# Pairing the value and gate projections: seven block products in place of eight on half of the k-tiles

## The chip, the cores and the metric

The kernel runs on one core of a Trainium2 chip. That core has five engines that run side by side, each working through its own list of instructions strictly in order: TensorE (PE) for matrix products, VectorE (DVE) and ScalarE (ACT) for elementwise work, GpSimd (POOL) and SyncE (SP), which here mostly issue DMA transfers. PE loads a stationary block of 128x128 (PEld in the profile) and streams a moving block of up to 512 columns past it; it accumulates into PSUM, which DVE and ACT read back into SBUF. The metric is the device time of one execution in microseconds, lower being better.

## The reference, cut to what matters

A sequence of 256 tokens of width 2048 passes through two layers. Each layer normalises the tokens, multiplies them by a wide input matrix, mixes over time per head, multiplies by a SiLU gate and projects back to 2048.

```python
# layer 0: gated linear attention, 4 heads
proj = h @ w_in                       # (256 x 2048) @ (2048 x 10240)
q, k, v, gate = jnp.split(proj, [1024, 2048, 2048 + 4096], axis=-1)
...                                   # decays, scores, o = scores @ v, per-head norm
return (o * jax.nn.silu(gate)) @ w_out            # (256 x 4096) @ (4096 x 2048)
# layer 1: retention, 8 heads
proj = h @ w_in                       # (256 x 2048) @ (2048 x 12288)
q, k, v, gate = jnp.split(proj, [2048, 4096, 4096 + 4096], axis=-1)
...                                   # rotary, scores * dmat, o = scores @ v, group norm
return (o * jax.nn.silu(gate)) @ w_out
```

All of it is float32. Nearly all of the arithmetic is in the four large products.

## The kernel before, in words

**Weights.** The host cuts the weights into groups of 512 columns; each group is 2048 rows, that is 16 k-tiles of 128 rows (`NKT`). A DMA on SP brings four k-tiles at a time into a tile `raw` (1 MB, three buffers, L110 to L118). To keep float32 accuracy with a one-pass matmul each weight is written as hi + lo: for two k-tiles at a time (a *sub*, `SUB` = 2, eight subs in a group), ACT copies the weights into `hi` with rounding (L151) and DVE subtracts, `lo = raw - hi` (L152), each an instruction over 128x1024 elements. `hi` and `lo` have three buffers each, and `LOOK` = 2 subs are split ahead of the one that PE is multiplying. The tokens are kept in the same form in `xhl` and `ogt`. A product is then three matmuls, hi·hi, hi·lo and lo·hi (`mm3`, L184 to L186).

**Groups.** `group_x` (L188) multiplies one weight group: for each sub, 2 k-tiles x 2 halves of 128 tokens x 3 matmuls of 512 columns, 12 in all, into two PSUM banks, one per half. `group_w` (L203) does the query and key group of a head, with weights stationary; its four results are brought back by `evac_w` (ACT L230, DVE L231).

**Heads.** A GLA head (`gla_head`, L575) has one `group_w`, then value group, gate group, value group, gate group. The value result is split into hi and lo by `v_evac` (L406, L407), the gate result goes through SiLU in `g_evac` (L415). A retention head (`ret_head`, L819) has one `group_w`, one value group and one gate group. After every two GLA heads and every four retention heads, `out_half` (L668) multiplies the gated output in `ogt` by four output groups and adds the result to `resid`, which stays in SBUF during the whole run.

**Order.** The smaller work (the decay and the scores of GLA `gla_scores`, L483; rotary and scores of retention `ret_scores`, L784; transposes `transpose_out`) is written as generators in a queue `side`; one step of it is taken after each sub by `advance`, and `drain_side` empties the queue at fixed places. `o_mms` (L418) multiplies scores by values, in a hook inside a later group. A scheduler that works on a timeline of its own then fixes the order on each engine; on the chip each engine follows that list and waits where an operand is not ready. PSUM is shared out as four banks `acc`, two `lev`, two `mis`.

Of the kernel before, what the change touches and what calls it, by code (L numbers as in the profile page):

```python
# [17 lines left out]
P = 128  # L18
# [7 lines left out]
CHUNK = 4  # L26
LOOK = 2
DMA_LOOK = 2
# [25 lines left out]

@with_exitstack
def kernel(
# [20 lines left out]
    raw_p = pool("raw", 3)  # L77
# [6 lines left out]
    sc_p = pool("sc", 2)  # L84
# [3 lines left out]
    acc_p = pool("acc", 4, space=psum)  # L88
    lev_p = pool("lev", 2, space=psum)
    mis_p = pool("mis", 2, space=psum)  # L90

# [6 lines left out]
    n_groups = w_all.shape[0]  # L98
    raws, splits = {}, {}
    emitted = {"raw": 0, "sub": 0}  # L100
    per_raw = CHUNK // SUB
    raws_per_group = NKT // CHUNK

    last0 = (n_groups - 1) * NSUB

    def emit_raw(parts=1):
        c = emitted["raw"]
        if c >= n_groups * raws_per_group:
            return
        t = raw_p.tile([P, CHUNK, GW], F32, tag="raw", name=f"raw{c}")  # L110
        g, j = divmod(c, raws_per_group)
        src = w_all[g, :, j * CHUNK * GW : (j + 1) * CHUNK * GW].rearrange("p (k n) -> p k n", n=GW)
        step = CHUNK // parts
# [24 lines left out]

    def emit_split(pieces=1):
        i = emitted["sub"]  # L140
        if i >= n_groups * NSUB:
            return
        c, j = divmod(i, per_raw)
        while emitted["raw"] <= min(c + DMA_LOOK, n_groups * raws_per_group - 1):
            emit_raw()
        src = raws[c][:, j * SUB : (j + 1) * SUB, :]
        hi, lo = split_tiles(i)
        step = SUB // pieces
        for k in range(pieces):
            sl = slice(k * step, (k + 1) * step)  # L150
            nc.scalar.activation(hi[:, sl], src[:, sl], AF.Copy)  # L151
            nc.vector.tensor_tensor(lo[:, sl], src[:, sl], hi[:, sl].bitcast(F32), ALU.subtract)  # L152
        splits[i] = (hi, lo)
        if j == per_raw - 1:
            del raws[c]
        emitted["sub"] += 1
# [17 lines left out]
    def next_weights():  # L174
        i = state["sub"]
        while emitted["sub"] <= min(i + LOOK, n_groups * NSUB - 1):
            emit_split()
        state["sub"] += 1
        return splits.pop(i)
# [8 lines left out]
    def group_x(lhs, name, hook=None, deadline=None, bank=None):  # L188
        bank = bank or (acc_p, "acc")
        ps = [bank[0].tile([P, GW], F32, tag=bank[1], name=f"{name}_ps{t}") for t in range(2)]  # L190
        for j in range(NSUB):
            if j == deadline:
                drain_side()
            hi, lo = next_weights()
            for q in range(SUB):
                for t in range(2):
                    mm3(ps[t], lhs, j * SUB + q, t, hi, lo, q)
            if hook is not None:
                hook(j)
            advance()  # L200
        return ps

    def group_w(rhs, name, extra=None):  # L203
        ps = [acc_p.tile([P, 2, SEQ], F32, tag="acc", name=f"{name}_ps{c}") for c in range(4)]
        for j in range(NSUB):
# [3 lines left out]
            if last:  # L209
                order = [(q, c) for c in range(4) for q in range(SUB)]  # L210
# [40 lines left out]
    resid = const([P, 2, D], "resid")  # L251
# [43 lines left out]
    w0 = emit_raw(4)  # L295
# [4 lines left out]
    w0(2)  # L300
    w0(3)
    x1 = load_xt(1)
    x1(0, 2)
    w1 = emit_raw(2)
    w1(0)
    x1(2, 4)
    w1(1)
    wa1_src = t4_p.tile([P, NKT, 16], F32, tag="qk", name="wa1_src", bufs=1)
    nc.sync.dma_start(wa1_src, w_a1)
    load_xt(2)(0, 4)  # L310
    emit_raw()
# [21 lines left out]
    def square_sum(t, c):  # L333
        junk = sg_p.tile([P, GW], F32, tag="sg", name="sqj")
        nc.scalar.activation(
            junk, resid[:, t, c * GW : (c + 1) * GW], AF.Square, accum_out=ssum[:, t, c : c + 1]
        )
# [5 lines left out]
    def first_group(j):  # L343
# [5 lines left out]
        if j == 1:  # L349
            load_xt(3)(0, 4)  # L350
        if j == 6:
# [22 lines left out]
    def gate_low_rank():  # L374
        for t in range(2):
            keep(nc.sync.dma_start(resid[:, t, :], x_n[:, t, :]))
            yield
        for c in range(8):
            square_sum(c // 4, c % 4)
            if c % 2:  # L380
                yield
# [21 lines left out]
    def v_evac(ps, r2, name):  # L403
        v = v_p.tile([P, 2, 2, GW], F32R, tag="v", name=name)
        for t in range(2):
            nc.scalar.activation(v[:, t, 0, :], ps[t], AF.Copy, scale=r2[:, t : t + 1])  # L406
            nc.vector.scalar_tensor_tensor(  # L407
                v[:, t, 1, :], ps[t], r2[:, t : t + 1], v[:, t, 0, :].bitcast(F32), ALU.mult, ALU.subtract
            )
        return v  # L410

    def g_evac(ps, r, name):
        sg = sg_p.tile([P, 2, GW], F32, tag="sg", name=name)
        for t in range(2):
            keep(nc.scalar.activation(sg[:, t, :], ps[t], AF.Silu, scale=r[:, t : t + 1]))  # L415
        return sg

    def o_mms(sc, v, name):  # L418
        ps = [acc_p.tile([P, GW], F32, tag="acc", name=f"{name}_ps{t}") for t in range(2)]
# [155 lines left out]
    def gla_head(h):  # L575
# [22 lines left out]
        def o_part(gi):  # L598
# [4 lines left out]
            o = o_p.tile([P, 2, GW], F32, tag="o", name=f"go{g}")  # L603
# [3 lines left out]
            os_.append(o)  # L607
# [28 lines left out]
        for gi in range(2):  # L636
            g = 2 * h + gi

            def v_hook(j):
                if h > 0 and gi == 1 and j == 1:  # L640
                    o_part(0)

            def g_hook(j):
                if h == 0 and gi == 1 and j == 5:
                    o_part(0)
                if gi == 1 and j == (6 if h == 0 else 2):
                    o_part(1)
# [4 lines left out]
            pv = group_x(xhl, f"gv{g}", v_hook)  # L652
            vs.append(v_evac(pv, r2, f"gv{g}"))
            sgs.append(g_evac(group_x(xhl, f"gg{g}", g_hook), r, f"gsg{g}"))
# [3 lines left out]
    def out_cols(c, ps, t, first, final):  # L658
        dst = resid[:, t, c * GW : (c + 1) * GW]
# [8 lines left out]
    def out_half(first, final, name):  # L668
        for c in range(4):
# [10 lines left out]
            for _ in transpose_out(  # L680
# [6 lines left out]
                pass  # L687

# [9 lines left out]
    def out_tail():  # L698
        kept = []
        half = GW // 2  # L700
        base = 3 * GW
        keep(nc.scalar.preload_act_table_set("natural_log_exp_and_others"))
        for t in range(2):
# [3 lines left out]
            ps = [acc_p.tile([P, half], F32, tag="acc", name=f"tail_ps{t}{n}") for n in range(2)]  # L707
# [111 lines left out]
    def ret_head(h):  # L819
# [11 lines left out]
        v = v_evac(group_x(xhl, f"rv{h}", bank=(lev_p, "lev")), r2, f"rv{h}")  # L831
# [5 lines left out]
        def o_part(j):  # L837
            if j != 2:
                return
            drain_side()  # L840
            po = o_mms(hw["sc"], v, f"ro{h}")
            o = o_p.tile([P, 2, GW], F32, tag="o", name=f"ro{h}")
# [18 lines left out]
            hw["o"] = o  # L861

        sg = g_evac(group_x(xhl, f"rg{h}", o_part), r, f"rsg{h}")
# [55 lines left out]
def _layout(i):  # L919
    gw, go = i["gla_w_in"][0], i["gla_w_out"][0]  # L920
    rw, ro = i["ret_w_in"][0], i["ret_w_out"][0]
    groups = []

    def add(a):
        groups.append(a.reshape(NKT, P, GW).transpose(1, 0, 2))

    def add_out(w, half):
        for c in range(4):
            add(w[half * D : (half + 1) * D, c * GW : (c + 1) * GW])

    for half in range(2):
        for h in (2 * half, 2 * half + 1):
            add(np.concatenate([gw[:, h * 256 : (h + 1) * 256], gw[:, 1024 + h * 256 : 1024 + (h + 1) * 256]], 1))
            for g in (2 * h, 2 * h + 1):
                add(gw[:, 2048 + g * GW : 2048 + (g + 1) * GW])
                add(gw[:, 6144 + g * GW : 6144 + (g + 1) * GW])
        add_out(go, half)
    for half in range(2):
        for h in range(4 * half, 4 * half + 4):
            add(np.concatenate([rw[:, h * 256 : (h + 1) * 256], rw[:, 2048 + h * 256 : 2048 + (h + 1) * 256]], 1))  # L940
            add(rw[:, 4096 + h * GW : 4096 + (h + 1) * GW])
            add(rw[:, 8192 + h * GW : 8192 + (h + 1) * GW])
        add_out(ro, half)
    w_all = np.empty((len(groups), P, NKT, GW), np.float32)
    for n, g in enumerate(groups):
        w_all[n] = g
# [14 lines left out]
        "w_all": w_all.reshape(len(groups), P, NKT * GW),  # L961
# [30 lines left out]
```

## Time and profile before

| what | value |
|---|---|
| time, median of 2 runs | 1443.36 us (1443.23 to 1443.49) |
| span of the profiled execution, first to last instruction | 1441.2 us |
| what lies around the span, median less span | 2.2 us |
| PE busy | 1429.9 us, 99% |
| DVE busy | 910.3 us, 63% |
| ACT busy | 690.0 us, 48% |
| DMA | 266.72 MB, mean 185 GB/s |
| granted TensorE clock, mean | 0.999 |

The busy times say what share of the span an engine had something under way. PE's matmuls overlap in the pipeline, so the duration of one matmul is longer than its share of the time: what one costs is the distance from one start to the next. In the groups of instructions each row has the line of the kernel, the engine, the operation, the written and the read tiles, the shape, the count, the busy time, the mean duration of one in ns, and the idle time just before with what ended it.

### The profile page before, as it was taken

To read this page: it belongs to the slowest core of one execution; us is meant where nothing else is said; L and a number is where in the kernel's file an instruction comes from. 1 tells how busy PE (TensorE), PEld (TensorE's weight loads), DVE (VectorE), ACT (ScalarE), POOL (GpSimd) and SP (SyncE) were. 2 spreads that over 40 slices of the span, in tenths; PEclk is the share of its full clock that TensorE was granted. 3 is DMA by queue.
4 is the path that set the end of the run, shared out by engine and by line. 5 is a ranking of instruction groups with operands and counts; after the bars stand their busy time and mean duration, and the time that the engine had idled before them with its cause. 6 is when DMAs were issued, how large, how long until landed. Compare 5 with 4: busy or idle time off the path is not lost.

```text
span 1441.2 us, 17504 instructions
## 1 busy us (share of the span) xinstructions
PE 1429.9 (99%) x6800; PEld 1181.0 (82%) x6800; DVE 910.3 (63%) x1430; ACT 690.0 (48%) x889; POOL 44.1 (3%) x98
## 2 busy tenths in 40 slices
PE   9999999999999999999999999999999999999997
PEld 6788888888888888888888888888888888888887
DVE  7595785545845764655666666664546666666654
ACT  4665654533554645454444444444344444444443
POOL 0010010000000010000000000000000000000000
PEclk9999999999999999999999999999999999999999
DMA  8643554555545555555555555555555555554562
GB/s 288 250 170 135 206 178 154 189 184 182 177 170 177 183 183 176 175 175 180 192 187 191 188 183 195 178 193 178 197 180 181 194 179 199 176 204 170 202 207 93
DMA packets 40499, 266.72 MB, mean 185 GB/s; under 512 B 4880, under 2 KB 5392, under 8 KB 9696
## 3 DMA queue, kind: packets, MB, share of 16 engines
q1 hardware_dynamic: 37536, 257.57, 51.2%
q0 software_dynamic: 2160, 6.95, 1.4%
q8 instruction: 53, 0.87, 0.2%
q10 hardware_dynamic: 720, 1.09, 0.2%
q14 instruction: 30, 0.25, 0.0%
HBM read 263.49 MB, written 2.10 MB: 184 GB/s over the span
## 4 chain that ended last, share of the span: by engine, by line
PE 99%; DMA 0%; SPq 0%; DVE 0%; ACT 0%; issue 0%
PE rqk_ps L219 8%; PE gv_ps L184 4%; PE gg_ps L185 4%; PE rv_ps L186 4%; PE gg_ps L186 4%; PE rv_ps L185 4%; PE rg_ps L185 4%; PE gv_ps L186 4%; PE rg_ps L186 4%; PE gv_ps L185 4%; PE rv_ps L184 4%; PE gg_ps L184 4%; PE rg_ps L184 4%; PE rqk_ps L220 4%; PE gqk_ps L219 4%; PE ra_ps L186 2%
## 5 line engine op out<-in xcount | busy, mean ns | idle before, releaser
L152 DVE TENSOR_TENSOR lo<-raw,hi 128x1024 fp32r<-128x1024 f32 (+1 forms) x473 | 577.6, 1223 | 439.9 <-ACT hi L151 421.5
L151 ACT ACTIVATE hi<-raw 128x1024 fp32r<-128x1024 f32 (+1 forms) x473 | 499.4, 1057 | 640.0 <-PE rg_ps L186 77.9
L219 PE MATMUL rqk_ps<-xhl,hi 128*128 128x512 f32 x480 | 165.9, 394 | 0.0
L220 PE MATMUL rqk_ps<-xhl,lo 128*128 128x256 f32 x480 | 127.2, 281 | 0.0
L219 PEld LDWEIGHTS rqk_ps<-xhl,hi 128*128 128x128 f32 x480 | 88.9, 188 | 16.1
L185 PE MATMUL gg_ps<-lo,xhl 128*128 128x512 f32 x256 | 102.1, 399 | 0.0
L185 PE MATMUL rv_ps<-lo,xhl 128*128 128x512 f32 x256 | 102.0, 399 | 0.0
L185 PE MATMUL gv_ps<-lo,xhl 128*128 128x512 f32 x256 | 102.0, 398 | 0.0
L186 PE MATMUL gv_ps<-hi,xhl 128*128 128x512 f32 x256 | 101.9, 398 | 0.0
L186 PE MATMUL gg_ps<-hi,xhl 128*128 128x512 f32 x256 | 101.7, 397 | 0.0
L186 PE MATMUL rv_ps<-hi,xhl 128*128 128x512 f32 x256 | 101.4, 396 | 0.0
L186 PE MATMUL rg_ps<-hi,xhl 128*128 128x512 f32 x256 | 101.3, 396 | 0.0
L185 PE MATMUL rg_ps<-lo,xhl 128*128 128x512 f32 x256 | 101.3, 396 | 0.0
L184 PE MATMUL gv_ps<-hi,xhl 128*128 128x512 f32 x256 | 94.7, 397 | 0.0
L184 PE MATMUL rv_ps<-hi,xhl 128*128 128x512 f32 x256 | 93.5, 396 | 0.0
L184 PE MATMUL rg_ps<-hi,xhl 128*128 128x512 f32 x256 | 93.5, 396 | 0.0
L184 PE MATMUL gg_ps<-hi,xhl 128*128 128x512 f32 x256 | 93.3, 397 | 0.0
L220 PEld LDWEIGHTS rqk_ps<-xhl,lo 128*128 128x128 f32 x480 | 89.2, 189 | 3.5
L219 PE MATMUL gqk_ps<-xhl,hi 128*128 128x512 f32 x240 | 80.0, 402 | 0.6 <-ACT hi L151 0.6
L220 PE MATMUL gqk_ps<-xhl,lo 128*128 128x256 f32 x240 | 57.6, 282 | 0.8 <-DVE lo L152 0.8
L186 PEld LDWEIGHTS rg_ps<-hi,xhl 128*128 128x128 f32 x256 | 48.1, 188 | 11.6
L185 PEld LDWEIGHTS rg_ps<-lo,xhl 128*128 128x128 f32 x256 | 48.1, 188 | 11.5
(265 smaller groups left out, 2395.2 us busy)
## 6 DMA issues: line engine op xcount, KB each, us to landing
raw<-in_w_all SPq DMA_DIRECT2D x238, 1024.0 KB, 4.8
resid<-in_x_n SPq DMA_DIRECT2D x2, 1024.0 KB, 7.8
gg<-in_gn_g POOLq DMA_DIRECT2D x8, 256.0 KB, 3.6
gb<-in_gn_b POOLq DMA_DIRECT2D x8, 256.0 KB, 4.5
dm<-in_dmat POOLq DMA_DIRECT2D x8, 192.0 KB, 2.6
raw<-in_w_all SPq DMA_DIRECT2D x4, 256.0 KB, 4.4
raw<-in_w_all SPq DMA_DIRECT2D x2, 512.0 KB, 7.3
xt<-in_x_t SPq DMA_DIRECT2D x2, 512.0 KB, 9.1
```

The costliest lines, as they stand in the source:

```text
L151: nc.scalar.activation(hi[:, sl], src[:, sl], AF.Copy)
L152: nc.vector.tensor_tensor(lo[:, sl], src[:, sl], hi[:, sl].bitcast(F32), ALU.subtract)
L184: mm(ps, xh, hi[:, q, :], start=kt == 0, stop=False)
L185: mm(ps, xh, lo[:, q, :], start=False, stop=False)
L186: mm(ps, xl, hi[:, q, :], start=False, stop=kt == NKT - 1)
L219: mm(ps[c], wh, rhs[:, kt, :, :], start=kt == 0, stop=False)
L220: mm(ps[c][:, 0, :], wl, rhs[:, kt, 0, :], start=False, stop=False)
```

## The change: what it does

For each GLA head part and each retention head, the value group V and the gate group G are now run together, by a new function `pair`. The product of X (256 tokens) by the 1024 columns of V and G is split by k: for k-tiles 8 to 15 it is as before (`normal`: 12 matmuls in a sub). For k-tiles 0 to 7, X is cut into four blocks (two token halves by two sets of four k-tiles) and the weights into four (V and G by the same two sets), and the eight block products are replaced by seven (`product`: 4 k-tiles x 3 matmuls for one token half, so 6 matmuls in a sub). Three of the products use plain token blocks, four use sums of token blocks; three use plain weight blocks and four use sums of weight blocks.

- The sums of tokens are made once for a layer by `make_sums` into `s` (16 KB per partition): 2 DVE additions over 128x1024, 4 over 128x512, and 4 splits over 512. They are written to DRAM and read back after the output half that follows (`reload_sums`).
- The sums of weights are made by DVE in `emit_adds`, in place in the loaded tiles: eight additions over 128x1024 for a pair (`use(..., add)` in `_plan`). Each block product has its own two subs to split, so a pair has 22 subs in place of 16.
- Partial results are kept by four ACT copies out of PSUM and combined by four DVE operations over 128x512. The value split and the SiLU come after that.
- `s` shares its SBUF space with the residual: `resid` is no longer kept in SBUF but read from DRAM before each `out_half` and written back after it, through the POOL queue (2 MB each way).
- Weights come in 512 KB transfers (two k-tiles); tiles that are used again by a sum have tags of their own (`x`, `y`, `z`, two buffers each) beside four `raw` buffers. `o_mms` takes its PSUM from `lev`; the four `acc` banks are handed out in rotation.

The core of the diff:

```diff
+    def pair(g, v):
+        def use(gid, js, add=None):
+            for j in js:
+                extra = None if add is None else last[add[0], add[1] + j % 2]
+                subs.append((last[gid, j], extra))
...
+        use(g, (0, 1))
+        use(g, (0, 1), (v, 0))
+        normal(v, 4)
+        for j in (2, 3):
+            load(v, j, "z")
+        use(g, (0, 1), (v, 2))
+        normal(v, 5)
+        use(v, (2, 3))
+        normal(v, 6)
+        use(v, (0, 1), (v, 2))
+        normal(v, 7)
+        for j in (2, 3):
+            load(g, j)
+        use(g, (2, 3))
+        normal(g, 4)
+        use(g, (0, 1), (g, 2))
+        for j in (5, 6, 7):
+            normal(g, j)
...
+    def emit_adds(upto):
+        while emitted["add"] <= min(upto, len(subs) - 1):
+            c, more = subs[emitted["add"]]
+            need = max(c, more or 0)
+            while emitted["raw"] <= min(need + DMA_LOOK, len(loads) - 1):
+                emit_raw()
+            if more is not None:
+                nc.vector.tensor_tensor(raws[c], raws[c], raws[more], ALU.add)
+            emitted["add"] += 1
...
+        def product(ps, left, stop=False):
+            for j in range(2):
+                hi, lo = next_weights()
+                for q in range(SUB):
+                    k = j * SUB + q
+                    three(ps, left(k, 0), left(k, 1), hi, lo, q, stop and k == QK - 1)
+            advance()
...
+        product(g1, plain(0, 0), stop=True)
+        keepf(sg[:, 0, :], g1)
+        product(v0, summed(1), stop=True)
+        keepf(o[:, 1, :], v0)
+        hook(0)
+        normal(v0, v1, 4, first=1)
+        hook(1)
+        product(g1, summed(2), stop=True)
+        keepf(o[:, 0, :], g1)
+        hook(2)
+        normal(v0, v1, 5)
+        hook(3)
+        product(v0, summed(0))
+        hook(4)
+        normal(v0, v1, 6)
+        hook(5)
+        product(g1, summed(3), stop=True)
+        keepf(sg[:, 1, :], g1)
+        tt(o[:, 1, :], o[:, 1, :], sg[:, 1, :], ALU.subtract)
+        hook(6)
+        normal(v0, v1, 7, stop=True)
+        tt(o[:, 0, :], v0, o[:, 0, :], ALU.subtract)
+        tt(o[:, 1, :], v1, o[:, 1, :], ALU.add)
+        on_v(v, o)
+        hook(7)
+        product(g0, plain(4, 0))
+        hook(8)
+        normal(g0, g1, 4)
+        hook(9)
+        product(g1, plain(4, 1))
...
+        normal(g0, g1, 7, stop=True)
+        tt(sg[:, 0, :], g0, sg[:, 0, :], ALU.add)
+        on_g(sg, [sg[:, 0, :], g1])
...
     def out_half(first, final, name):
+        get_resid(f"{name}_resid")
...
+        if not final:
+            put_resid(f"{name}_sum")
...
     out_half(True, False, "ga")
+    reload_sums("sums_a2")
...
     out_half(False, False, "gb")
+    side.append(make_sums(xhl, "sums_r"))
...
     out_half(True, False, "ra")
+    reload_sums("sums_r2")
```

More of the change, by code (lines that the diff above doesn't have):

```diff
@@ L96, in const, with acc @@
         return one.tile(shape, dtype, tag=name, name=name)
-    n_groups = w_all.shape[0]
+    loads, subs = _plan()
     raws, splits = {}, {}
[L100 to L104, printed above, removed]
+    emitted = {"raw": 0, "add": 0, "sub": 0}
+    last0 = len(subs) - NSUB
+    slots = deque(range(4))
+    def acc(n, name, shape=(P, GW)):
+        out = []
+        for i in range(n):
+            k = slots.popleft()
+            slots.append(k)
+            out.append(acc_p.tile(list(shape), F32, tag=f"acc{k}", name=f"{name}{i}"))
+        return out
     def emit_raw(parts=1):
         c = emitted["raw"]
[L108 to L113, printed above, removed]
+        tag = loads[c][2]
+        kw = {} if tag == "raw" else {"bufs": 2}
+        t = raw_p.tile([P, SUB, GW], F32, tag=tag, name=f"raw_{tag}{c}", **kw)
+        src = w_all[c].rearrange("p (k n) -> p k n", n=GW)
+        step = SUB // parts
         raws[c] = t
@@ L310 @@
     load_xt(2)(0, 4)
+    emit_raw()
     emit_raw()
```

288 lines of the change are left out of this document (196 added, 92 removed).

## The prediction

> **What bounds the kernel now.** I read the page from the top: busy times, slices, the chain that ended last.
>
> ```profile
> span 1441.2 us, 17504 instructions
> PE 1429.9 (99%) x6800; PEld 1181.0 (82%) x6800; DVE 910.3 (63%) x1430; ACT 690.0 (48%) x889; POOL 44.1 (3%) x98
> ...
> PE   9999999999999999999999999999999999999997
> ...
> DVE  7595785545845764655666666664546666666654
> ...
> PE 99%; DMA 0%; SPq 0%; DVE 0%; ACT 0%; issue 0%
> ```
>
> PE bounds every stage, and nothing else is on the chain. VectorE has room on the mean, but in the first 16 slices, the GLA layer, it reaches 7 and 8 tenths. A busy PE doesn't say what a matmul costs; the chain in order of time does (start, length, what), and its later rows give the length of a retention head.
>
> ```profile
> 22.44 0.93 PE gqk_ps L219 x4
> ...
> 763.74 0.93 PE rqk_ps L219 x4
> 834.91 0.93 PE rqk_ps L219 x4
> 906.09 0.93 PE rqk_ps L219 x4
> ```
>
> Four matmuls of 512 columns take 0.93 us, 0.2325 each; so 12 matmuls, a sub of `group_x`, take 2.79 us, and a retention head 71.17. VectorE's load in such a head and in GLA heads 1, 2 and 3 (start and end; length; busy time and count of PE, PEld, DVE, ACT, POOL; clock; DMA share; GB/s):
>
> ```profile
> 763.74:834.91 71.17, 71.17 (x349) 59.46 (x348) 46.58 (x68) 31.62 (x40) 1.61 (x3) 1.00 0.54 187
> ...
> 142.65:271.30 128.65, 128.65 (x606) 106.00 (x606) 94.90 (x187) 72.30 (x103) 7.20 (x16) 1.00 0.53 181
> 355.40:473.86 118.46, 118.46 (x562) 97.82 (x561) 75.73 (x142) 62.51 (x82) 7.44 (x16) 1.00 0.51 180
> 473.86:596.02 122.16, 122.16 (x578) 100.63 (x577) 80.57 (x149) 65.91 (x88) 6.86 (x15) 1.00 0.51 176
> ```
>
> DVE has 24.6 us left in a retention head, and 33.8, 42.7 and 41.6 in the GLA heads. What it costs when it works without a pause is in its timeline (start, length, instruction): the distance from start to start.
>
> ```profile
> 704.69 1.23 DVE L152 TENSOR_TENSOR lo<-raw,hi 128x1024 fp32r<-128x1024 f32 x1 [1.55 <-ACT hi L151]
> 705.83 1.50 DVE L231 TENSOR_TENSOR rqk<-rqk_ps,rqk_h 128x256 f32<-128x256 f32 x4
> 707.37 1.23 DVE L790 TENSOR_TENSOR ra<-rqk,trig 128x1024 f32<-128x1024 f32 x1
> 708.51 0.69 DVE L791 TENSOR_TENSOR rb<-rqk,trig 128x512 f32<-128x512 f32 x1
> 709.11 0.69 DVE L793 TENSOR_TENSOR rb<-rqk,trig 128x512 f32<-128x512 f32 x1
> ...
> 169.27 0.29 DVE L529 TENSOR_TENSOR w<-lc 128x128 f32<-128x128 f32 x1
> 169.47 0.29 DVE L530 TENSOR_TENSOR w<-lc 128x128 f32<-128x128 f32 x1
> ```
>
> So 1.14 us for 1024 elements, 0.60 for 512, 0.20 for 128, and 1.54 for the four of `evac_w`.
>
> **The change part by part.**
>
> *PE.* A pair has 7 x 12 + 96 = 180 matmuls for 192. 16 pairs save 192 of them: 192 x 0.2325 = **-44.6 us**, 2.79 in each pair. PE is on the chain throughout, so this comes back in full unless PE then waits.
>
> *VectorE.* Per pair 6 more splits, 8 sums of weights and 4 combining operations: 14 x 1.14 + 4 x 0.60 = 18.4 us, where PE gets 2.79 shorter. A sum over 128x1024 stands nowhere in this trace in place; its nearest row is the split L152, two SBUF operands of the same shape, at 1.14 from start to start and 1.23 long when the next has to wait. I take 1.14. On the mean a retention head then has 46.6 + 18.4 = 65.0 us of DVE work beside 71.17 - 2.79 = 68.4 of PE. GLA heads 1, 2 and 3 have two pairs: 131.7, 112.5 and 117.4 beside 123.1, 112.9 and 116.6. So head 1 alone is over by 8.6, head 3 by 0.8; the rest would fit, if the work were spread evenly. It isn't, and that decides.
>
> *Where DVE comes late, retention.* `hi` and `lo` have three buffers, so the split of a sub begins at the earliest when PE has ended the sub three before: DVE starts on a pair with two subs of PE's old work in hand, 2 x 2.79 = 5.6 us. In the order of DVE's instructions in the built program there stand, up to the end of the split for the pair's eighth sub: 8 splits and 7 sums (15 x 1.14 = 17.1), `evac_w` (1.54), and of `ret_scores` one operation of 1024 elements, five of 512 and one of 256 (1.14 + 3.0 + 0.4): 23.2 us. A sub of a block product lasts only 6 x 0.2325 = 1.4 us, so PE is through the seven subs before in 6 x 1.4 + 2.79 = 11.2, and some 1.2 for the score matmuls (ten of 128 or 256 columns, half a 512's time each, an estimate). The first matmul of a sub needs only `hi`: 0.2. PE waits 23.2 - 5.6 - 11.2 - 1.2 - 0.2 = **5.0 us in each of 8 heads, +40**. Afterwards PE has full subs again and DVE catches up, so it is not paid twice.
>
> *GLA.* The score work stands, in each head, in one pair's list. Its rows by form:
>
> ```profile
> L534 DVE TENSOR_TENSOR w<-w,qk 128x128 f32<-128x128 f32 x56 | 16.8, 300 | 0.0
> L533 DVE TENSOR_TENSOR w<-w,qk 128x128 f32<-128x128 f32 x56 | 16.8, 299 | 0.7 <-ACT w L531 0.7
> L530 DVE TENSOR_TENSOR w<-lc 128x128 f32<-128x128 f32 x56 | 16.6, 296 | 0.0
> L529 DVE TENSOR_TENSOR w<-lc 128x128 f32<-128x128 f32 x52 | 15.4, 295 | 0.5 <-PE lv L495 0.5
> ```
>
> That is 56 in a head (with the `ref` form of L529), 11.2 us at 0.20, and some 5 for the rest of it (an estimate: about eight operations of 256 to 512 elements). Up to the seventeenth split DVE has 25 x 1.14 + 1.54 + 16.2 + 3 x 0.60 (combining) = 48.0. PE has 12 x 1.4 + 4 x 2.79 = 28.0 for the sixteen subs before and about 2.2 for twenty score matmuls. The wait: 48.0 - 28.0 - 2.2 - 5.6 - 0.2 = 12.0 us, in four heads **+48**. Two more pairs are loaded: the first of all takes the sums of tokens (2 x 1.14 + 8 x 0.60 = 7.1), the last of head 1 the rotary tables (16 operations over 256 elements and ten small ones, about 8). Without side work a pair comes out even (15 x 1.14 = 17.1 by its eighth split, for 5.6 + 11.2 + 0.2), so most of these is waited for: **+11**.
>
> *ACT.* 6 x 1.06 + 4 x 0.67 = 9.0 us more in a pair by the two rows below, 145 in all, 835 busy out of about 1500: no bound. A copy out of PSUM has the other half's six matmuls (1.4 us) or more as cover; if a split (1.06) stands ahead of it, it is late by 0.3, at most 5 us over 16 pairs. I take 0. A summed tile passes DVE, ACT, DVE: where nothing else stood between, DVE would lose 1.06. The built order has another split or side operation there nearly always; 0, and for one in four of 128 sums 34.
>
> ```profile
> L151 ACT ACTIVATE hi<-raw 128x1024 fp32r<-128x1024 f32 x471 | 498.2, 1059 | 637.4 <-PE rg_ps L186 77.9 <-PE rqk_ps L219 77.1 <-PE gg_ps L186 73.5
> L605 ACT ACTIVATE go<-go_ps,rr 128x512 f32<-128x512 f32 x16 | 10.6, 674 | 0.0
> ```
>
> *DMA.* The weights' bytes are the same, in halves. New are 2 MB transfers on POOL's queue: residual in and out, token sums out and in. Reading has an output group (22.3 us) as cover. Three places are tighter. Twice the residual goes out and the sums come in before the second block product, with `group_w` and one product, 22.3 + 2.8 us, as cover; once, at the layer's change, new sums wait until the residual has left, with three subs, 8.4 us, as cover, and they stand ahead of splits on DVE and ACT. Prices:
>
> ```profile
> raw<-in_w_all SPq DMA_DIRECT2D x238, 1024.0 KB, 4.8
> resid<-in_x_n SPq DMA_DIRECT2D x2, 1024.0 KB, 7.8
> 8.00:16.00 8.00, 6.53 (x36) 5.22 (x35) 6.53 (x13) 3.48 (x4) 0.95 (x1) 1.00 1.02 389
> ```
>
> At 7.8 us a megabyte a transfer takes 15.6: late by 6 twice and by 7 once, 19 us. Beside the weights' 187 GB/s the engines have 389 - 187 = 202 GB/s left, 10.4 us: late by 2 once. I take **+2**, ends 0 and 19. [...] No run so far has this transfer. At the start, more loads stand ahead of the first group's last subs in a stretch that is short of DMA (the row above): **+2**.
>
> *Sum.* -44.6 + 40 + 48 + 11 + 2 + 2 = +58.4; 1441.2 + 58.4 = 1499.6 of span, and 2.2 around it as before (1443.36 - 1441.2): **1502 us**, 4% slower. A run of this kernel can tell about 2% from no change.
>
> **The rivals.**
>
> *A, PE stays the bound; faster.* Price: -44.6 + 8.6 + 0.8 from the means, 1406 + 2 = **1408 us**. The mechanism is side work sliding into the parts where DVE has room (`group_w`, and a pair's last four subs). It decides from the point where no more than 23.2 - 5.0 = 18.2 us of DVE work stands ahead of a retention pair's eighth split. For it: the means fit nearly everywhere. Against it: DVE takes its list in order, and all 23.2 stand there.
>
> *B, DVE is dearer than its start-to-start rows.* If each large operation took its 1.23 us, 15 per retention head and 25 per GLA score pair cost 0.09 more each: 8 x 1.35 + 4 x 2.25 = 20; with the ACT link for one sum in four, 34 more: **1522 to 1556**. For it: sums hang on earlier sums in the same tile. Against: the rows above. [...]
>
> *C, the lead is larger.* If DVE had three subs in hand, 2.8 us less in each of 14 loaded stretches: 1502 - 39 = **1463**. Against: three buffers, one of which PE is reading.
>
> *D, the transfers are late,* by their upper price: **1519**.
>
> *E, waiting costs PE its clock.* The start shows short waits (idle time in brackets):
>
> ```profile
> 9.93 1.20 PE L219 MATMUL gqk_ps<-xhl,hi 128*128 128x512 f32 x4 [0.65 <-ACT hi L151]
> 11.95 0.74 PE L220 MATMUL gqk_ps<-xhl,lo 128*128 128x256 f32 x4 [0.82 <-DVE lo L152]
> ```
>
> The 8:16 row has them at a clock of 1.00. Waits come here sub by sub, 1 to 4 us, mostly under 2.4, so I price it at 0. [...]
>
> That the change doesn't save what it says is excluded: the built program has 6524 matmuls for 6716.
>
> **How the numbers follow.** The forecast, with D beside it, has 0.66; A 0.06; C and what lies towards A 0.14, half of it within 2%; B 0.14. The range is 1463 (C) to 1548 (most of B). Faster by over 2% (under 1414) 0.06; within 2% (to 1472) 0.12; slower 0.82.
>
> **What would show it.** In the profile after: 192 fewer matmuls; DVE near 85% busy and 9 tenths in the GLA layer; PE idle 90 to 110 us, ended by DVE on `lo`, in the first half of the pairs, none in the output groups; retention heads of 73 to 74 us; rows for the sums of 1.2 us. It is wrong if PE's idle time is small, or is ended by ACT or DMA, or if the sums take another time than the splits.

## The result and the profile after

The changed kernel takes **1541.68 us** (median of 2 runs, 1540.90 to 1542.47) for 1443.36 before: a ratio of 1.068 (95% interval 1.065 to 1.071), 6.8% slower. Forecast was 1502, with a range up to 1548. From the page of the changed kernel, the lines that answer to those of before:

```profile
span 1540.6 us, 18316 instructions
...
PE 1441.1 (94%) x6608; PEld 1158.8 (75%) x6608; DVE 1199.6 (78%) x1738; ACT 821.9 (53%) x1056; POOL 70.1 (5%) x109
...
PE   8898988999989988999999999999998989898997
...
DVE  7899798854898798866697879786448797979754
...
PEclk9899998999999999999999999999999999999999
...
PE 70%; DVE 19%; issue 4%; ACT 3%; DMA 3%; POOL 1%; SPq 0%; DVEq 0%; ACTq 0%; POOLq 0%
```

There are 192 fewer matmuls, but PE's busy time didn't fall: 1441.1 for 1429.9, where 44.6 us less were to be expected. Beside that PE stands idle for 1540.6 - 1441.1 = 99.5 us (before: 1441.2 - 1429.9 = 11.3). VectorE now has 19% of the chain that ended last. The clock row, all nines before, has two eights: the second thing to look at.

PE's waits, and those of its weight loads (columns: who waited for whom, us in total, times, longest):

```profile
PE re_ps L300 <- DVE lo L237: 23.6, 10, 2.6
PE ga_ps L300 <- DVE lo L237: 22.5, 30, 2.0
PE ga_ps L299 <- ACT hi L236: 12.4, 15, 4.5
PE ga_ps L299 <- DVE qk L438: 9.4, 3, 7.4
```
```profile
PEld ga_ps L300 <- DVE lo L237: 38.4, 46, 2.4
```

About half of the 99.5 us is ended by DVE's splits in the pairs (`ga`, `re`): 23.6 + 22.5 = 46.1. ScalarE's copies there (`hi`) end 16.7, and 15.2 are spent on projections that DVE has not yet brought out of PSUM (`qk`, `rqk`). In the chain that ended last ScalarE has only 3%. The weight loads wait longer than the matmuls, so a part of the waiting lies inside PE's busy time. The sums of weights are as long as a split, in the groups of instructions by form (count, busy time, mean ns):

```profile
L237 DVE TENSOR_TENSOR lo<-raw_x,hi 128x1024 fp32r<-128x1024 f32 x128 | 156.6, 1224 | 20.6 <-ACT hi L236 20.6
L223 DVE TENSOR_TENSOR raw_x<-raw_x,raw_raw 128x1024 f32<-128x1024 f32 x32 | 39.2, 1225 | 10.5 <-DMA raw_raw<-in_w_all 10.5
```

By stage (start and end; length; busy time and count of PE, PEld, DVE, ACT, POOL; clock; DMA share; GB/s), cut where the first projections of the first GLA head and of the first retention head leave PSUM; first the two layers of before, behind a start of 33.9 us, then the three stages of after:

```profile
33.90:705.83 671.93, 671.93 (x3142) 552.32 (x3140) 428.86 (x754) 356.03 (x479) 27.84 (x61) 1.00 0.52 180
705.83:1441.20 735.37, 727.32 (x3516) 605.36 (x3514) 457.13 (x633) 319.83 (x393) 12.89 (x24) 1.00 0.53 184
```
```profile
0.00:45.59 45.59, 32.26 (x148) 23.71 (x148) 35.01 (x58) 17.97 (x25) 3.51 (x13) 0.96 0.78 279
45.59:770.32 724.73, 680.23 (x3044) 540.53 (x3044) 572.69 (x908) 420.00 (x560) 51.58 (x68) 0.98 0.58 187
770.32:1540.60 770.28, 728.58 (x3416) 594.59 (x3416) 591.87 (x775) 383.98 (x472) 15.06 (x28) 0.97 0.58 184
```

Each layer should have lost 22.3 us of matmuls (8 pairs of 2.79). Against that the start is 11.7 us longer, GLA 724.7 - (671.9 - 22.3) = 75.1, retention 770.3 - (735.4 - 22.3) = 57.2: 144 us, of which the prediction had 103 (4, 59 and 40).

Most of the other 41 stands in the clock column. The second retention head in two stretches, and its middle in windows of 2 us (same columns):

```profile
844.90:863.90 19.00, 15.06 (x55) 11.38 (x56) 18.55 (x24) 9.10 (x12) 0.00 (x0) 0.82 0.09 28
863.90:921.10 57.20, 56.90 (x282) 47.48 (x280) 45.31 (x64) 30.52 (x39) 1.61 (x3) 1.00 0.72 224
```
```profile
851.00:853.00 2.00, 0.00 (x0) 0.00 (x0) 2.00 (x2) 0.00 (x0) 0.00 (x0) 1.00 0.00 0
853.00:855.00 2.00, 1.44 (x5) 0.86 (x5) 2.00 (x3) 0.60 (x1) 0.00 (x0) 0.87 0.00 0
855.00:857.00 2.00, 1.49 (x4) 1.20 (x5) 2.00 (x4) 1.28 (x3) 0.00 (x0) 0.50 0.28 35
857.00:859.00 2.00, 2.00 (x6) 1.61 (x5) 2.00 (x3) 1.65 (x3) 0.00 (x0) 0.50 0.57 227
859.00:861.00 2.00, 2.00 (x6) 1.52 (x5) 2.00 (x4) 0.00 (x0) 0.00 (x0) 0.50 0.00 0
861.00:863.00 2.00, 2.00 (x12) 1.74 (x12) 1.93 (x2) 1.09 (x2) 0.00 (x0) 0.92 0.00 0
```

and the chain in order of time there (start, length, what):

```profile
853.71 0.23 PE re_ps L301
...
856.31 0.43 PE re_ps L300
...
860.57 0.43 PE re_ps L301
...
862.01 0.23 PE re_ps L301
```

All but 0.3 us of the head's idle time lies in its first stretch, 3.9 us. DVE is busy there almost without a pause, PE stands still for 2.6 us from 850.6 on, and soon after its clock is halved: a matmul takes 0.43 us for 0.23. From 857 on PE no longer waits, and still it works at half speed until 861.3. Added up over windows of 6 us (length times one less the granted clock) this comes to **39.1 us** in the whole run, 1.8 before. The mean clock says the same: 0.975 over 1540.6 us is 38.5. By stage, in windows of 1 us, it is 1.7, 17.0 and 20.5, of which the last 1.7 lie behind the last output group, as before.

This sum is an upper bound, because it also counts stretches of half clock in which PE had nothing to do. The longest wait of the run, 7.4 us for the first head's projections, has such a stretch:

```profile
42.00:48.00 6.00, 1.84 (x4) 1.50 (x5) 6.00 (x11) 1.19 (x3) 0.00 (x0) 0.51 0.28 87
```

Weighted in each window by PE's busy share, so that only slow work counts, the clock costs 31.6 us: nothing in the start, 14.2 in GLA and 17.3 in retention; before, nothing.

### The profile page after: what moved, and what is told of

Read it like the earlier page. It is cut to its first block, busy times and chain, and to the rows that moved or that the text cites. A ratio compares the mean times of both kernels' runs of the same rounds, so it can differ in the third digit from the quotient of the medians.

```text
span 1540.6 us, 18316 instructions
## 1 busy us (share of the span) xinstructions
PE 1441.1 (94%) x6608; PEld 1158.8 (75%) x6608; DVE 1199.6 (78%) x1738; ACT 821.9 (53%) x1056; POOL 70.1 (5%) x109
## 4 chain that ended last, share of the span: by engine, by line
PE 70%; DVE 19%; issue 4%; ACT 3%; DMA 3%; POOL 1%; SPq 0%; DVEq 0%; ACTq 0%; POOLq 0%
DVE lo L237 8%; PE re_ps L300 6%; PE re_ps L301 6%; PE re_ps L299 6%; PE rqk_ps L426 6%; PE ga_ps L300 4%; PE ga_ps L301 4%; PE ga_ps L299 4%; PE rqk_ps L427 3%; DVE raw_x L223 3%; PE gqk_ps L426 2%; PE ra_ps L269 2%; PE ga_ps L268 2%; PE gb_ps L267 2%; PE ra_ps L267 2%
## 5 line engine op out<-in xcount | busy, mean ns | idle before, releaser
L237 DVE TENSOR_TENSOR lo<-raw_raw,hi 128x1024 fp32r<-128x1024 f32 x375 | 457.1, 1224 | 245.0 <-ACT hi L236 242.9
L236 ACT ACTIVATE hi<-raw_raw 128x1024 fp32r<-128x1024 f32 x375 | 396.2, 1059 | 437.1 <-PE re_ps L301 94.8
L236 ACT ACTIVATE hi<-raw_x 128x1024 fp32r<-128x1024 f32 (+1 forms) x130 | 136.3, 1049 | 135.6 <-DVE raw_x L223 54.2
L237 DVE TENSOR_TENSOR lo<-raw_x,hi 128x1024 fp32r<-128x1024 f32 (+1 forms) x130 | 158.0, 1216 | 21.2 <-ACT hi L236 21.2
L300 PE MATMUL ga_ps<-lo,xhl 128*128 128x512 f32 x352 | 145.4, 413 | 12.1 <-DVE lo L237 11.9
L299 PE MATMUL ga_ps<-hi,xhl 128*128 128x512 f32 x352 | 136.5, 411 | 17.1 <-DVE qk L438 9.4
L300 PE MATMUL re_ps<-lo,xhl 128*128 128x512 f32 x352 | 144.5, 411 | 0.1
L301 PE MATMUL re_ps<-hi,xhl 128*128 128x512 f32 x352 | 143.4, 407 | 0.0
L301 PE MATMUL ga_ps<-hi,xhl 128*128 128x512 f32 x352 | 142.5, 405 | 0.0
L299 PE MATMUL re_ps<-hi,xhl 128*128 128x512 f32 x352 | 133.6, 409 | 5.8 <-DVE rqk L438 5.8
L299 PEld LDWEIGHTS ga_ps<-hi,xhl 128*128 128x128 f32 x352 | 67.6, 193 | 37.0 <-ACT hi L236 11.3
L300 PEld LDWEIGHTS ga_ps<-lo,xhl 128*128 128x128 f32 x352 | 68.1, 194 | 35.2 <-DVE lo L237 20.4
L299 PEld LDWEIGHTS re_ps<-hi,xhl 128*128 128x128 f32 x352 | 68.3, 194 | 26.2 <-DVE rqk L438 8.3
L301 PEld LDWEIGHTS re_ps<-hi,xhl 128*128 128x128 f32 x352 | 69.1, 196 | 16.8
L301 PEld LDWEIGHTS ga_ps<-hi,xhl 128*128 128x128 f32 x352 | 68.2, 194 | 15.1
L300 PE MATMUL re_ps<-lo,sums_r 128*128 128x512 f32 x128 | 53.3, 417 | 23.6 <-DVE lo L237 23.6
```

The costliest lines, as they stand in the source:

```text
L299: mm(ps, xh, hi[:, q, :], start=start, stop=False, **again)
L300: mm(ps, xh, lo[:, q, :], start=False, stop=False, **again)
L301: mm(ps, xl, hi[:, q, :], start=False, stop=stop, **again)
```

## The experiments

Theory 1: VectorE comes late in the pairs, because it works its list in order and is never more than two subs ahead; and the waits halve PE's clock besides. Rivals: the frame around the pairs (transfers, halves of loads, turns of PSUM; theory 2), and a VectorE that is simply too full or too dear (theory 3). PE idle is span less busy time and the clock's cost is the sum over all windows, the upper bound of above, both of the profiled execution; a head is the distance between the `evac_w` of two retention heads.

| run | us | ratio to before, 95% interval | PE idle | clock's cost | retention head |
|---|---|---|---|---|---|
| before | 1443.4 | | 11.3 | 1.8 | 71.2 |
| after | 1541.7 | 1.068, 1.065 to 1.071 | 99.5 | 39.1 | 74.4 to 76.5 |
| no sums | 1451.6 | 1.005, 1.003 to 1.007 | 48.0 | 8.7 | 70.2 |
| eight products | 1452.8 | 1.006, 1.005 to 1.008 | 16.9 | 5.8 | 71.6 to 72.2 |
| side work late | 1559.7 | 1.080, 1.079 to 1.082 | 109.1 | 50.4 | 74.7 to 75.7 |
| filled with three | 1609.3 | 1.115, 1.113 to 1.116 | 59.5 | 14.4 | 79.9 |
| filled with one | 1562.9 | 1.082, 1.080 to 1.084 | 84.5 | 26.5 | 76.4 to 77.3 |
| sums in order | 1541.4 | 1.068, 1.066 to 1.069 | 96.5 | 41.8 | 74.5 to 75.1 |
| sums on GpSimd | 1655.8 | 1.147, 1.145 to 1.149 | 195.4 | 77.7 | 80.9 to 82.1 |
| half sums | 1489.5 | 1.031, 1.030 to 1.033 | 67.3 | 17.1 | 71.1 to 72.6 |
| four buffers, two for loads | 1651.9 | 1.145, 1.141 to 1.148 | 167.1 | 68.9 | 78.4 to 84.0 |
| four buffers, with room | 1503.6 | 1.041, 1.039 to 1.043 | 85.4 | 20.8 | 71.4 to 71.5 |
| five buffers, with room | 1494.1 | 1.035, 1.033 to 1.036 | 80.5 | 35.2 | 69.5 |
| retention only | 1448.2 | 1.003, 1.002 to 1.004 | 33.1 | 11.0 | 69.5, the first 71.1 |

### Without the sums of weights

```diff
-            if more is not None:
-                nc.vector.tensor_tensor(raws[c], raws[c], raws[more], ALU.add)
```

> Leaves out the eight sums of weights in each pair; the products that should use them use the first weight block alone, so the output is another one. Everything else of the change stays: 22 splits in a pair, the seven products, loads in halves, the 2 MB transfers. Theory 1 (VectorE's list ahead of a pair's first half is too long, and the waits halve TensorE's clock besides): the list gets 7 x 1.14 = 8.0 us shorter up to a retention pair's eighth split, 15.2 for the 18.2 that decide, so retention no longer waits; GLA's two loaded pairs keep about 48.0 - 9.1 - 36.0 = 2.9 us each. 1408 + 4 x 2.9 + 11 at the start = 1425 to 1445, matmuls at 0.23 us nearly everywhere. Theory 2 (the frame: transfers, halves of loads, turns of PSUM): over 1500, since none of that is touched. Theory 3 (a split costs more in the new order): 1480 or more.

1451.6: 90 us of the 98 are gone with 128 instructions, and the clock's cost falls to 8.7. The frame can't be the cause, and neither can a dearer split: the splits are all still there. It is 6.6 us over what theory 1 expected: a retention head is 70.2, not the 68.4 of its matmuls, mostly since PE still waits 1.4 us in each, now for ScalarE's copy `hi`.

### Eight products in the new frame

```diff
-        product(g1, plain(0, 0), stop=True)
...
+        for j in range(NSUB):
+            normal(v0, v1, j, stop=j == NSUB - 1)
...
+        for j in range(NSUB):
+            normal(g0, g1, j, stop=j == NSUB - 1)
```

> Keeps what the change put around the pairs (value and gate in one pair, 2 MB transfers for residual and token sums, which are made and moved but not used, PSUM turns, value out of PSUM by ScalarE) and computes all sixteen subs of a pair with eight block products as before, without sums of weights. The output is the reference's. Theory 1: 6800 matmuls again and no long list, so 1443 plus a start of 2 to 11 us: 1445 to 1460, no row of VectorE ending PE's idle time with more than 10 us. Theory 2 (the frame makes the time): 1490 to 1540, with PE's idle time ended by DMA or by ScalarE's copies.

1452.8, as theory 1 expected. In the list of PE's waits the longest row is

```profile
PE ga_ps L281 <- DVE qk L395: 3.5, 3, 3.1
```

The frame with its 2 MB transfers costs 9.2 us, 3.2 of it at the start. Rival D of the prediction falls with it.

### The side work later

```diff
+        def step():
+            calls[0] += 1
+            if calls[0] > 8 or name == "ga0":
+                advance()
...
-        nc.vector.tensor_tensor(a, qk, tb(0, 4), ALU.mult)
+        keep(nc.vector.tensor_tensor(a, qk, tb(0, 4), ALU.mult))
...
-                nc.vector.tensor_tensor(raws[c], raws[c], raws[more], ALU.add)
+                keep(nc.vector.tensor_tensor(raws[c], raws[c], raws[more], ALU.add))
```

> The whole change, but the side work (scores of GLA and retention) is held back on VectorE's list until the second half of a pair, and each sum stands right ahead of the split that needs it. Ahead of a retention pair's eighth split there then stand 8 splits, 3 or 4 sums and the four operations that take projections out of PSUM, 14 to 15 us where 18.2 decide. Theory 1: retention pairs no longer wait in their first half (heads of 69 to 71 us for 74 to 76), GLA's waits shrink to a third, 1420 to 1470. Theory 3 (VectorE is simply full, the order matters little): waits move to the second half, and the time stays within 20 us of 1541. Theory 2: 1541.

1559.7: the expectation of theory 1 was wrong, and that of theory 3 came true (waits in the second half, within 20 us of 1541). Three stretches of the second retention head (columns as above):

```profile
862.60:881.35 18.75, 18.14 (x78) 14.09 (x77) 17.23 (x19) 12.63 (x15) 0.00 (x0) 1.00 0.22 65
881.35:887.60 6.25, 6.25 (x29) 5.08 (x28) 5.17 (x5) 4.08 (x5) 0.00 (x0) 1.00 0.97 358
887.60:906.35 18.75, 14.74 (x64) 11.20 (x64) 17.88 (x23) 9.40 (x12) 0.54 (x1) 1.00 0.59 182
```

The first stretch has 0.6 us of idle time, where the changed kernel has 3.9 in its first 19. That agrees with the point that was worked out: no wait with less than 18.2 us ahead of the eighth split. But the waits stand in the third stretch instead, 4.0 us, where the side work now is. The order moves the wait; it doesn't remove it. What the list meets is a store of two subs, 5.6 us at most, that can't be filled further while DVE has time: a burst is waited for wherever it stands beside short subs. This run can't tell such a store from a VectorE that is too full; the runs with more lead below do, for retention.

### Filling the waits

```diff
+        def fill(hi):
+            count[0] += 1
+            if count[0] > 13:
+                return
+            for _ in range(3):
+                keep(mm(g0, lhs[:, 0, 0, 0:P], hi[:, 0, :], start=True, stop=True, skip_group_check=True))
```

> The whole change, and in each pair three more matmuls of 512 columns after each of the first 13 subs, into a PSUM bank that is not yet in use and is overwritten later (624 matmuls, 0.7 us a sub at full clock, 145 us if none of it fell into waits). The output is the reference's. Theory 1 has two parts, waiting for VectorE (about 60 us) and a clock that falls after the waits (about 38 us). If the clock falls because TensorE stands still, the fill holds it up: matmuls at 0.23 us in the loaded stretches, mean clock over 0.99. The waits are only filled there; pairs with little side work pay up to 9 us each. 1500 to 1560. If the clock fell for another reason (power, VectorE's traffic), matmuls of 0.43 us stay and the time is 1600 or more.

The time, 1609, is outside what theory 1 expected and in the range of the other reading, but the sign by which the two were to be told apart, the clock, is theory 1's. The same place in the head, windows of 6.7 us:

```profile
885.80:892.46 6.66, 6.20 (x27) 5.03 (x28) 6.66 (x11) 3.71 (x5) 0.00 (x0) 1.00 0.00 0
892.46:899.12 6.66, 5.33 (x26) 4.14 (x25) 6.66 (x8) 2.48 (x4) 0.00 (x0) 1.00 0.08 19
```

Clock 1.00 where it was halved, with DVE as busy as before, 6.66 us of 6.66. No window of 1 us in the eight retention heads is below 1.00. So here it is standing still that costs the clock, not VectorE's traffic. 145 us of matmuls were added; 40 took the place of idle time and at most 25 came back from the clock, which leaves 80, and 68 were measured; the difference of 12 stays open.

With one matmul in place of three:

```diff
-            for _ in range(3):
+            for _ in range(1):
```

> As the filled run, with one more matmul a sub in place of three (0.2325 us, 208 in all, 48 us at most). Filling three gave 1609: 145 us of matmuls for 68 of time, the clock at 1.00 in the retention heads. If the clock depends on how much TensorE stands still (theory 1), one matmul takes only 3 us of a pair's first part and leaves most of the waits: the clock loss lies between 39 us (none) and 14 (three), 20 to 39, and the time at 1541 + 48 less what falls into waits and less the clock won, 1530 to 1570. If any work between waits keeps the clock, its loss goes to 14 and the time to 1515 to 1535.

1562.9: 48 us added, 15 of idle time and 12.6 of clock less, 20.8 left; 21.2 measured (16.5 between the two profiled executions). With the fills the clock's cost goes down with the idle time: 99.5 us of it cost 39, 84.5 cost 26.5, 59.5 cost 14.4. It is no fixed price: the table has 85.4 at 20.8 and 80.5 at 35.2.

### Sums in order, and on GpSimd

```diff
-                nc.vector.tensor_tensor(raws[c], raws[c], raws[more], ALU.add)
+                keep(nc.vector.tensor_tensor(raws[c], raws[c], raws[more], ALU.add))
```

> The whole change; each sum of weights is held at its place in the program, right ahead of the split that needs it, and can't be moved ahead of earlier splits on VectorE. Side work stays where the change has it. At the start this takes the sum that waits for its load out of the way of the first group's last splits: the first head's projections come out at about 41 us, as in the run with late side work, for 45.6 (4.6 us less). In the pairs, theory 1 (VectorE holds only two subs of work in hand, 5.6 us, and any burst beyond that is waited for) sees no gain, since the same work stands ahead of the pair's eighth split but for one or two sums (1 to 2 us in a retention head): 1520 to 1540. If a summed tile's way from VectorE to ScalarE and back is what costs (a sum right ahead of its split has no cover), heads get longer by some 2 us: 1545 to 1575.

1541.4, just outside what theory 1 expected. The first projections come at 41.0 us, 4.6 earlier, so the sum that waits for its load does hold up the first group; the first GLA head gives it back (141.4 us to the next head for 134.6). A sum right ahead of its split costs nothing that shows.

```diff
-                nc.vector.tensor_tensor(raws[c], raws[c], raws[more], ALU.add)
+                nc.gpsimd.tensor_tensor(raws[c], raws[c], raws[more], ALU.add)
```

> The whole change, with the eight sums of a pair made by GpSimd in place of VectorE. The run without sums gives the floor: 1451. If VectorE's time is what the sums cost, and GpSimd's work lies beside it, 1451 to 1475, mean clock 0.99. If GpSimd's sums take over 3 us each, or slow VectorE's own operations, or PE waits for GpSimd by name: 1500 to 1600.

1655.8, slower by another 114 us. GpSimd takes 2.7 to 3.4 us for a sum, by the means of its four groups, and VectorE's operations beside it get longer (groups by form):

```profile
L1018 DVE TENSOR_TENSOR rqs<-ra,rqs 128x512 fp32r<-128x512 f32 x8 | 23.0, 2881 | 0.0
```

The operation, on 512 elements, took 690 ns in the changed kernel; the 2881 ns here are as long as one of GpSimd's sums. What holds it up for that long was not shown.

### Half the sums

```diff
-                nc.vector.tensor_tensor(raws[c], raws[c], raws[more], ALU.add)
+                nc.vector.tensor_tensor(
+                    raws[c][:, :, 0 : GW // 2], raws[c][:, :, 0 : GW // 2], raws[more][:, :, 0 : GW // 2], ALU.add
+                )
```

> The whole change, with each sum of weights made over 256 of its 512 columns (the other half stays unsummed, so the output is another one): as many instructions, with the same waits and the same order of data, at about 0.60 us for 1.14. If the time of the sums in VectorE's list is the cost (theory 1), 8 x 0.54 = 4.3 us a pair goes of the 9.1 that were worth 90 us (1541.7 to 1451.6): 1485 to 1505. If it is the link (a sum, then ScalarE's copy, then the split) or the number of instructions, 1525 to 1541.

1489.5: 47% of the sums' time is gone, and 52 of the 90 us with it, with as many instructions and links as in the changed kernel. So it is the sums' time in VectorE's list that costs.

### More lead

```diff
-LOOK = 2
+LOOK = 3
...
-    raw_p = pool("raw", 4)
-    hi_p = pool("hi", 3)
-    lo_p = pool("lo", 3)
+    raw_p = pool("raw", 2)
+    hi_p = pool("hi", 4)
+    lo_p = pool("lo", 4)
```

> The whole change, with four buffers for each half of a split in place of three, and one more sub looked ahead; SBUF has the room only if loads get two buffers in place of four. Theory 1: VectorE has three subs in hand, 8.4 us for 5.6, so each of some 14 loaded stretches waits 2.8 us less, and most of the 39 us of clock comes back with it: 1541 - 39 - 20 to 39 = 1463 to 1485, if two load buffers suffice. If they don't, PE's or ScalarE's idle time is ended by DMA, and the time is 1500 or more. Theory 3 (VectorE is full on the mean, lead doesn't help): 1530 or more without waits on DMA.

1651.9, and it tells nothing of the lead: two load buffers don't suffice. From the waits:

```profile
ACT hi L236 <- DMA raw_raw<-in_w_all: 462.5, 244, 8.5
```

With all four load buffers kept, and four buffers for `hi` and `lo` (`LOOK` = 3) or five (`LOOK` = 4):

```diff
+    def __getitem__(self, ix):
+        return self.t[(ix[0], ix[1] % (NKT // 2)) + tuple(ix[2:])]
...
-    ogt = const([P, NKT, 2, SEQ], "ogt", F32R)
+    ogt = Folded(const([P, NKT // 2, 2, SEQ], "ogt", F32R))
```

> The whole change with four buffers for each half of a split and one more sub looked ahead, as in the run before, but with all four load buffers kept: the room in SBUF comes from storing only eight of the sixteen k-tiles of the heads' transposed outputs, later heads writing over earlier ones, so the output is another one, while every operation, transfer and matmul stays. Theory 1 (two subs in hand are too few for the bursts): each of some 14 loaded stretches waits 2.8 us less, 39 us, and the clock lost there comes back in part: 1463 to 1495. Theory 3 (VectorE is full on the mean of each pair, and lead only moves the wait): 1520 to 1545.

> As the run before it with five buffers and two more subs looked ahead than the change has. Theory 1: another step of 2.8 us in the stretches that still wait (GLA's 12.0 by the prediction, retention's 5.0 are covered): 1425 to 1465, retention heads of 69 to 71 us, clock over 0.99. Theory 3: 1520 to 1545.

1503.6 and 1494.1: between the two theories, and each is right for one layer. Retention heads go from 74.4 to 76.5 us to 71.5 and 69.5, with no half clock inside them; here the second head with five buffers in two stretches:

```profile
837.10:856.10 19.00, 18.52 (x83) 15.20 (x84) 19.00 (x24) 12.86 (x16) 0.00 (x0) 1.00 0.43 135
856.10:906.60 50.50, 49.85 (x254) 41.92 (x252) 44.13 (x63) 26.48 (x35) 1.61 (x3) 1.00 0.66 214
```

Twice 2.8 us more in hand would be 5.6; 4.2 of idle time and 3.4 of clock were there to be won in the second head, and 6.7 were. So theory 3 is out for retention. GLA is hardly shorter (716 and 718 us for 725): with five buffers PE's idle time in that stage is still 718.4 - 673.7 = 44.7 us (44.5 in the changed kernel), and the clock's cost there is 26 (17). Only the waits are others, of five buffers:

```profile
PE ga_ps L307 <- DVE qk L446: 15.2, 5, 12.0
PE got_tp L656 <- DVE ga_o L842: 14.3, 4, 8.2
...
PE go_ps L645 <- ACT sc L672: 10.9, 3, 5.7
```

PE waits for the results of side work themselves and for projections that leave PSUM late; no store of splits helps against that. The first row was 9.4 in the changed kernel, and the second had no row there. That they come later because more splits stand ahead of them is only argued, and a VectorE that is too full stays a rival for GLA.

### Retention only, with five buffers and the whole output

```diff
-            pair(("ag", g), ("av", g))
+            for gid in (("av", g), ("ag", g)):
+                plain(gid)
...
+        if ret0 <= i < last0 and turn == 3:
+            both = spare("v", 1, [2, SUB, GW], f"both{i}", F32R)
+            return both[:, 0], both[:, 1]
+        if ret0 <= i < last0 and turn == 4:
+            return spare("sg", 1, [SUB, GW], f"hi{i}", F32R), spare("o", 1, [SUB, GW], f"lo{i}", F32R)
```

> Seven products in the retention heads alone; GLA's pairs are computed with eight, as in the run with eight products, and no sums of tokens are made for that layer. In the retention layer the splits have five buffers: the second buffers of value, gate and output tiles, which only GLA needs in pairs, hold the two more, so that the room is there and the output is the reference's. Theory 1: retention heads of 69.5 us as in the run with most lead, for 71.2 before, 8 x 1.7 = 14 us less; GLA and the start as in the run with eight products, 2 to 7 us more than before: 1430 to 1440, faster than before by 0.3 to 1%. If what the lead won was won by the folded outputs and not by the buffers, the heads stay at 74 us or more: 1460 or more.

1448.2, not faster, and outside the 1430 to 1440 that theory 1 expected. By stage, cut as above:

```profile
0.00:43.40 43.40, 32.69 (x146) 24.89 (x146) 24.58 (x46) 14.43 (x19) 4.16 (x14) 0.88 0.91 334
43.40:724.24 680.84, 675.16 (x3144) 553.19 (x3142) 439.64 (x770) 374.50 (x506) 31.95 (x65) 1.00 0.60 190
724.24:1446.70 722.46, 705.77 (x3416) 587.39 (x3416) 583.33 (x771) 379.66 (x468) 15.10 (x28) 0.99 0.59 196
```

The retention layer, with the change and five buffers, takes 722.5 us for 735.4 before: 12.9 less, heads of 69.5, as theory 1 expected, and without the folded outputs. The start (9.5 longer, with PE waiting 7.0 for `xhl`) and GLA (8.9 longer) give it back. In that wait VectorE, which makes `xhl`, itself waits 2.7 and 3.3 us for loads of tokens, and the start's clock of 0.88 (1.00 before) shows half clock behind it. Why the loads come later than in the run with eight products, whose start took 37.1, stays open; a version with the start of the kernel before and this retention layer was not run.

## Why the prediction came out as it did

**Direction and mechanism held; one term was priced at nothing.** The forecast was 39.7 us too low. The term that failed is rival E, "waiting costs PE its clock", priced at 0 because waits would be "1 to 4 us, mostly under 2.4". It measured 31.6 us of slow work (39.1 - 1.8 = 37.3 as upper bound); the start makes up nearly all of the rest (below). The row that E went by (short waits at the start at a clock of 1.00) had waits of 0.65 and 0.82; those in the pairs reach 2.6 us in retention and 4.5 in GLA. In the trace of before no matmul but the first waited longer than 0.82 us, so what a wait of 1 to 4 us costs stood in no row, and the 0 for it was the author's estimate. The filled runs show the cause: with matmuls put into the waits the clock's cost falls from 39.1 to 26.5 and 14.4 us. A clock halved while PE stands idle does stand at the end of the trace of before: PE's last matmul there ends at about 1433.2, and from about 1437.6 on the clock is halved:

```profile
1437.00:1441.20 4.20, 0.00 (x0) 0.00 (x0) 0.00 (x0) 0.00 (x0) 0.00 (x0) 0.57 0.63 235
```

In the changed kernel the clock fell after a wait of 2.6 us: in the second retention head PE stands still from 850.6 to 853.2, and from about 854.5 on the clock is halved, for 6.8 us (below).

**PE, -44.6.** Right: 6608 matmuls for 6800, at 0.23 us wherever the clock is whole.

**VectorE's prices.** Right: sums take 1.22 us, and 1.13 to the next start in the chain of the second head; rival B's 0.09 more per operation doesn't show. One sign was wrong by the prediction's own prices: VectorE is 78% busy (572.69 of 724.73 in GLA, 79%), where it names near 85% and nine tenths; (910.3 + 16 x 18.4 + 2 x 7.1) / 1499.6 is 81%.

**Retention, +40.** Stage loss 57.2 less 17.3 of slow work: 39.9. The place is right too: 3.9 of the 4.2 us of idle time of the second head lie in its first 19 us. Heads of 73 to 74 us became 74.4 to 76.5, with a clock's cost of 1.7 or 3.4 us in each.

**GLA, +48 and +11.** 75.1 less 14.2: 60.9. The sum is right, the sorting only in part: of the 44.5 us that PE stands idle in this stage `lo` ends 22.5, but ScalarE's `hi` ends 12.4, which the prediction didn't have. So the fit of the sum may in part be luck.

**The start, +2.** Mis-sized: 11.7, of which PE waits 7.4 for the first head's projections. DVE's in-order list has a sum of weights, moved ahead by the scheduler, that waits for its load in front of splits of the first group; holding it back won 4.6, and 3.2 are there with eight products as well. The rest stays open.

**ACT, 0, and the transfers, +2.** The transfers cost nothing that shows: no row of PE's waits names one of residual or sums, which took 6.7 to 11.3 us for 2 MB, beside an estimate of 10.4. ScalarE's copies do end 16.7 us of PE's waits in the pairs, which by the prediction was a sign against it. Half the sums on VectorE's list took 52 us away with the links as they were, so VectorE is behind most of the loss; how much is ScalarE's own was not separated.

**The rivals.** A stood on side work sliding to where VectorE has room. It was put there, its point was met, and the wait moved along. C's three subs in hand were not what the kernel had, but made so they give what C claimed in retention, and not in GLA.

## What to carry to other kernels

A saving on the bound engine that is paid on an engine with 37% of idle time is still a loss when that idle time can't be stored: ask how much finished work the buffers hold (here two subs, 5.6 us), and compare the longest burst with it, not the busy shares. A wait on TensorE was dearer here than its length, 32 us of slow work beside 99 of idle time: add the clock. Where buffers can be found for the stage alone (five for three), the same change did win 12.9 us in the retention layer, though the run as a whole was not faster.

## What the runs showed of the hardware that was not expected

- The half clock came in stretches of about 3.4 us and multiples of it: in windows of 1 us the changed kernel has fourteen ahead of its end, of 3.4, 6.8 and 10.2 us. A short one in a window of 6 us:

```profile
456.00:462.00 6.00, 4.72 (x14) 3.63 (x15) 2.92 (x3) 3.47 (x5) 0.67 (x3) 0.72 0.59 183
```

  Here 6 x 0.28 / 0.5 = 3.4 us were run at half speed; in the head above, from 853 to 863, 2 x (0.13 + 0.50 + 0.50 + 0.50 + 0.08) / 0.5 = 6.8. There a wait of 2.6 us and a shorter one behind it cost about 3 us more than themselves.
- GpSimd's sums over 128x1024 stretch VectorE's operations over 128x512 at the head of a retention pair to four times (690 to 2881 ns); its splits of summed tiles, which mostly follow a sum, take 1571 ns on average for 1224. GpSimd's small score operations (128x64) take 480 ns before, 453 with eight products, 836 after and 900 without the sums of weights, so those sums don't slow them; what does stays open.
